# Moving GpSimd's long steps to VectorE and ScalarE, layer-2 SiLU as ScalarE's function, new costs in the order generator, and two table loads

## The chip, the core and the metric

The kernel runs on one core of one Trainium2 chip. A core has five engines that run side by side and wait for each other by semaphores: TensorE (PE, matmuls), VectorE (DVE), ScalarE (ACT), GpSimd (POOL) and SyncE (SP, which issues the transfers). The metric is the device time of one launch in microseconds; lower is better.

## What is computed

A sequence of 2048 frames of width 1024 (float32) passes through two layers and a final RMSNorm. Each layer scales and shifts the normalised frames by a condition vector `c`, mixes them along the sequence, gates them and adds them to the residual stream.

```python
def reference(x, c, ada_w, ada_b, norm_g, final_g, ...):
    c_act = jax.nn.silu(c)
    for i in range(2):
        cond = c_act @ ada_w[i] + ada_b[i]                 # shift, scale, gate: 3 x 1024
        h = rmsnorm(x, norm_g[i]) * (1.0 + scale) + shift
        if i == 0:
            out = rglru_block(h, ...)                      # layer 1
        else:
            out = gated_deltanet_block(h, ...)             # layer 2
        x = x + gate * out
    return rmsnorm(x, final_g)

def rglru_block(h, ...):
    xb, zg = split(h @ in_w)                               # 1024 -> 2 x 1024
    xb = causal_dwconv(xb, conv_w) + conv_b                # 4 taps along the sequence
    r_t, i_t = sigmoid(blockwise(xb) @ gate_w + gate_b)    # 8 blocks of 128
    log_a = -8.0 * r_t * softplus(-lam)
    a_t, b_t = exp(log_a), sqrt(-expm1(2.0 * log_a)) * (i_t * xb)
    hseq = scan(h_t = a_t * h_(t-1) + b_t)
    return (hseq * silu(zg)) @ out_w

def gated_deltanet_block(h, ...):
    q, k, v, z, a_in, b_in = split(h @ in_w)               # 8 heads of 128; z: gate
    q, k, v = silu(causal_dwconv((q, k, v), conv_w))
    q, k = l2norm(q) * 128 ** -0.5, l2norm(k)
    beta, g = sigmoid(b_in), -exp(a_log) * softplus(a_in + dt_bias)
    o = chunk_gated_delta_rule(q, k, v, g, beta)           # state 128 x 128 per head
    return (rmsnorm(o) * onorm_g * silu(z)) @ out_w
```

## The kernel before

**Matmuls in three products.** Each float32 operand of a large matmul is split in an upper half, rounded by a cast to the matmul's reduced type, and a lower half, the operand minus the upper half. PE makes three products of the halves (`products`, L668): upper by upper, upper by lower, lower by upper.

**Tiles and stages.** The sequence is cut in two units (u = 0, 1) of 1024 frames, each unit in two tiles (i = 0, 1) of 512. Layer 1 projects each tile with 16 weight panels of 1024 x 128 (kinds x and z, 8 each), layer 2 with 32 (k, v, q, z). A panel is loaded once per unit (L606), its upper half is cast on ACT (`whi`, L644). In the first unit the lower half is made on POOL (`wlo`, L650) and also stored; in the second unit it is loaded back. A projected tile of 128 x 512 is then worked on by ACT, DVE and POOL while PE goes on:

- layer 1, x: convolution (`convolve`, L746 on ACT, L756 on DVE), halves of the result (`xh` L798 on ACT, `xl` L801 on DVE), gate matmuls (`pg`, L807), sigmoids as tanh on ACT (L857), then `gates_thread`: tanh and exp on ACT (L817, L819), two DVE steps (L821, L823), one POOL step (`th`, L825), DVE (L827), square root on ACT (L830), DVE product (L834), scan on DVE (L838), and the product with the gate `tz` on POOL (L845), then the store to `y_d`.
- layer 1, z: tanh on ACT (L783) and (tanh + 1) times the input on DVE (L785): SiLU, up to a factor of two that the output weights take up.
- layer 2, k, v, q (`conv2_thread`): a copy out of PSUM on ACT (`xe`, L730), the first tap on POOL (`xf`, L997), three taps on DVE (L718), tanh on ACT (L1009) and (tanh + 1) times the input on DVE (L1014). The convolution's weights are halved beforehand (L379), so this is SiLU.
- layer 2, z (`zgate_thread`): tanh (L1023) and a DVE step (L1025), then a store.
- layer 2, keys (`key_thread`): four exponentials of the decays on ACT per tile and head (L1128), transposed keys (`pk`, L1135), their norms with a power on POOL (`rsqrt`, L242 and L243), products of keys (`pkk`).
- layer 2, inverses: a 32 x 32 triangular inverse in 31 pairs of small DVE steps (L1292, L1295), and four rounds of small matmuls.
- layer 2, recurrence: per 128 frames `pp` on PE (L1412, L1413), `zt` on DVE (L1421), `py` on PE (L1429), `yt` on ACT (L1435), `pS` on PE (L1441, L1442), `state` on DVE (L1454).

Where a tile of activations is made for a projection (`split_thread`), ACT scales and shifts it (L561), the upper half is cast on DVE (L569; for the first four on ACT, L566), and the lower half is made on DVE (L575) or, for the first four and for every odd one of the later tiles, on POOL (L572).

At the start, `first_loads_thread` loads the condition's weights (L292) for layer 1 in four pieces, one after the other; two of them go through PE (L328), two through DVE (L353, L355), and PE sums the latter over the partitions (L277). `columns_thread` loads eight small tables (L374) after the second piece and prepares them on DVE (L379 to L389, softplus in L248 to L260); three more small tables come earlier (L303). The later condition rows are summed on DVE (L410).

**What sets the order.** Engines execute their instructions in the order in which the program writes them. That order comes from a generator in the kernel's source (`Weave`): each step of the work is a small thread that asks for an engine with a duration (`yield "dve", 0.33`), for a buffer, or for an event. The generator keeps a time for each engine, always takes the step that can start earliest (by priority where equal), and writes its instruction. After a step, the thread goes on at the step's end plus a lag per engine, or plus a lag given at that place. These durations only set the order; they change nothing in the instructions themselves.

## Time and profile before

| | us |
|---|---|
| runs, lowest, median, highest | 1934.42, 1935.67, 1940.69 |
| span of the profiled execution | 1937.1 |
| busy: PE, DVE, ACT, POOL | 1844.0, 1471.2, 1048.2, 654.8 |

The profile is one execution. "Busy" is the time in which an engine had an instruction in work; matmuls overlap each other, so a busy PE is not a PE at its peak. A line of a group gives the kernel's line, engine, operation, the tile written and the tiles read, the count, busy time, mean duration in nanoseconds, and the idle time of the engine just before with what ended it. A line of the timeline gives the start, the duration, and the same names. Stages by the trace: the start up to 50 us, layer 1 up to 500, its output projection up to 668, layer 2's first unit up to 1240, its second up to 1745, the last projection to the end.

### The profile page before, as it was taken

The numbers are of one execution on the slowest core, as the hardware profiler recorded it, in microseconds if no ns is written. First come the engines' busy times: TensorE is split into PE (matmuls) and PEld (weight loads), VectorE is DVE, ScalarE is ACT, GpSimd is POOL, SyncE is SP. The second block draws the span as 40 slices with busy tenths as digits, with TensorE's granted clock in tenths as the row PEclk, the third lists the DMA queues.
The fourth block names the chain that finished last, engine by engine and source line by source line (L and its number), as shares of the span: only waits on it lengthen the run. The fifth ranks groups of instructions, "written<-read, shape, count | busy, mean of one in ns | idle before, by whom it ended". The sixth has DMA issues, their size and how long they took to land.

```text
span 1937.1 us, 31289 instructions
## 1 busy us (share of the span) xinstructions
PE 1844.0 (95%) x10286; PEld 1503.9 (78%) x10286; DVE 1471.2 (76%) x3175; ACT 1048.2 (54%) x2587; POOL 654.8 (34%) x1116
## 2 busy tenths in 40 slices
PE   6999999999899999898999999999999999999998
PEld 3787778878688877677787877788888888888887
DVE  6898998887544668869888896769777878886653
ACT  3666677667212345375565663565666656654321
POOL 3344542223100235345445543333332334411110
PEclk9999999999899999999999998999999999999999
DMA  8476746554578735446676565555365555687751
GB/s 320 116 219 189 223 138 220 175 167 138 169 204 236 208 106 145 128 111 160 166 186 141 138 158 150 149 156 158 102 163 143 140 140 139 155 246 207 230 161 66
DMA packets 511723, 322.77 MB, mean 167 GB/s; under 512 B 371268, under 2 KB 439236, under 8 KB 511560
## 3 DMA queue, kind: packets, MB, share of 16 engines
q1 hardware_dynamic: 511560, 320.77, 59.1%
q8 instruction: 81, 1.33, 0.3%
q14 instruction: 82, 0.67, 0.1%
HBM read 219.93 MB, written 100.73 MB: 166 GB/s over the span
## 4 chain that ended last, share of the span: by engine, by line
PE 61%; DVE 20%; DMA 6%; issue 4%; ACT 4%; SPq 3%; POOL 2%; DVEq 0%; POOLq 0%; ACTq 0%
PE mm L668 31%; PE mmo L668 16%; DVE xf L718 2%; DVE ttmp L1292 2%; DVE tblk L1295 2%; PE pg L807 1%; PE py L1429 1%; PE pp L1412 1%; PE pS L1442 1%; PE pqk L1257 1%; PE pS L1441 1%; PE pp L1413 1%; PE pkk L1169 1%; DVE xf L756 1%; DMA raw<-in_w 1%
## 5 line engine op out<-in xcount | busy, mean ns | idle before, releaser
L718 DVE SCALAR_TENSOR_TENSOR xf<-xe,cw_s,xf 128x512 f32<-128x512 f32 x288 | 224.9, 784 | 20.6 <-POOL xf L997 18.1
L650 POOL TENSOR_TENSOR wlo<-raw,whi 128x1024 fp32r<-128x1024 f32 x48 | 120.9, 2519 | 143.6 <-ACT whi L644 115.4
L1292 DVE TENSOR_TENSOR ttmp<-blk,tblk 128x60 f32<-128x60 f32 (+24 forms) x496 | 125.4, 253 | 16.6 <-DMA blk<-blk_d 5.4
L1295 DVE TENSOR_TENSOR tblk<-tblk,ttmp 128x60 f32<-128x60 f32 (+24 forms) x496 | 124.8, 252 | 10.7
L644 ACT CAST whi<-raw 128x1024 fp32r<-128x1024 f32 x96 | 100.2, 1044 | 50.3 <-DMA raw<-in_w 44.5
L668 PE MATMUL mmo<-oh,yh 128*128 128x512 f32 x256 | 102.1, 399 | 4.8 <-ACT oh L907 4.8
L668 PE MATMUL mm<-hh_('in2', 0)_5342,whi 128*128 128x512 f32 x256 | 105.3, 411 | 0.0
L668 PE MATMUL mm<-hh_('in2', 0)_5437,whi 128*128 128x512 f32 x256 | 105.3, 411 | 0.0
L668 PE MATMUL mmo<-ol,yh 128*128 128x512 f32 x256 | 102.2, 399 | 3.0 <-DVE ol L909 3.0
L668 PE MATMUL mm<-hh_('in2', 0)_5342,wlo 128*128 128x512 f32 x256 | 104.7, 409 | 0.0
L668 PE MATMUL mm<-hl_('in2', 0)_5343,whi 128*128 128x512 f32 x256 | 104.7, 409 | 0.0
L668 PE MATMUL mm<-hl_('in2', 0)_5438,whi 128*128 128x512 f32 x256 | 104.1, 407 | 0.0
L668 PE MATMUL mm<-hh_('in2', 1)_12030,wlo 128*128 128x512 f32 x256 | 104.1, 407 | 0.0
L668 PE MATMUL mm<-hl_('in2', 1)_12219,whi 128*128 128x512 f32 x256 | 104.0, 406 | 0.0
L668 PE MATMUL mm<-hh_('in2', 0)_5437,wlo 128*128 128x512 f32 x256 | 103.9, 406 | 0.0
L668 PE MATMUL mm<-hh_('in2', 1)_12218,whi 128*128 128x512 f32 x256 | 103.6, 405 | 0.0
L668 PE MATMUL mm<-hh_('in2', 1)_12030,whi 128*128 128x512 f32 x256 | 103.5, 404 | 0.0
L668 PE MATMUL mm<-hl_('in2', 1)_12031,whi 128*128 128x512 f32 x256 | 103.3, 403 | 0.0
L668 PE MATMUL mm<-hh_('in2', 1)_12218,wlo 128*128 128x512 f32 x256 | 103.2, 403 | 0.0
L668 PE MATMUL mmo<-ol,oh 128*128 128x512 f32 (+1 forms) x264 | 103.1, 391 | 0.0
L668 PE MATMUL mmo<-oh,ol 128*128 128x512 f32 (+1 forms) x264 | 103.1, 391 | 0.0
L668 PE MATMUL mmo<-oh,oh 128*128 128x512 f32 (+1 forms) x264 | 103.0, 390 | 0.0
(331 smaller groups left out, 5649.8 us busy)
## 6 DMA issues: line engine op xcount, KB each, us to landing
raw<-in_w SPq DMA_DIRECT2D x96, 512.0 KB, 4.2
araw<-in_ada_w SPq DMA_DIRECT2D x32, 512.0 KB, 4.3
xt<-x_d SPq DMA_DIRECT2D x32, 512.0 KB, 4.9
xt_d<-xb SPq DMA_DIRECT2D x192, 64.0 KB, 2.4
xk<-xt_d SPq DMA_DIRECT2D x24, 512.0 KB, 6.1
xt<-in_x SPq DMA_DIRECT2D x16, 512.0 KB, 4.4
ada<-in_ada_w SPq DMA_DIRECT2D x16, 512.0 KB, 8.5
y_d<-tz SPq DMA_DIRECT2D x32, 256.0 KB, 3.2
```

The source lines that it names most:

```text
L644: act.copy(hi, raw)
L650: pool.tensor_tensor(lo, raw, f(hi), ALU.subtract)
L668: pe.matmul(pt, lhsT=lhs[a][:, k, :], rhs=rhs[b][:, k, :], start=(k == 0 and n == 0), stop=(k == KT - 1 and n == 2))
L718: dve.scalar_tensor_tensor(xf, xe[:, 1 + j:1 + j + TC], wc[:, j:j + 1], xf, ALU.mult, ALU.add)
L756: dve.scalar_tensor_tensor(xf[:, 3:TC], pt[:, j:j + TC - 3], wc[:, j:j + 1], xf[:, 3:TC], ALU.mult, ALU.add)
L807: pe.matmul(pg, lhsT=a[:, g, :], rhs=b, start=(q == 0), stop=(q == 2))
L1169: pe.matmul(pkk[:, b, :], lhsT=kc, rhs=kc, start=True, stop=True)
L1257: pe.matmul(pqk[:, b, :], lhsT=kt[:, b * P:(b + 1) * P], rhs=qt[:, b * P:(b + 1) * P], start=True, stop=True)
L1292: dve.tensor_tensor(tmp, blk[:, j, j + 1:32].unsqueeze(2).to_broadcast([P, r, c_]), t[:, j, 0:c_].unsqueeze(1).to_broadcast([P, r, c_]), A ...
L1295: dve.tensor_tensor(t[:, j + 1:32, 0:c_], t[:, j + 1:32, 0:c_], tmp, ALU.subtract)
L1412: pe.matmul(pp[:, 0, :], lhsT=kc, rhs=S_, start=True, stop=True)
L1413: pe.matmul(pp[:, 1, :], lhsT=qc, rhs=S_, start=True, stop=True)
```

## The change

1. **Work moves.** The lower half of a weight panel, the lower halves of the activations and layer 1's product with the gate go from POOL to DVE. The first tap of layer 2's convolution goes from POOL to ACT. Layer 2's SiLU becomes one ACT instruction with the function Silu, in place of tanh on ACT and a DVE step; the halving of the convolution's weights and of the output norm's factor goes with it. POOL keeps the powers, the carries of the convolution, the masks, one step of layer 1's decay (L825) and the lower half of the gate weights (L875).
2. **Loads at the start.** Eleven small tables become two (`head`, `small`), packed on the host. The first weight panel is loaded before the condition's weights, and these come in alternating pieces for PE and DVE. The tables are prepared on DVE as soon as `c` is spread out.
3. **The generator.** Durations and lags are new numbers throughout. A step named `dve2` or `pool2` is not placed inside a step of the other kind. A step of ACT can name its table ("exp", "silu", "sqrt"); a change of table costs 1.28. PE pays 0.12 where a thread comes to it from a wait. The durations of large matmuls go from 0.2163 (layer 2) and 0.2275 (layer 1) to 0.228.
4. **Small ones.** The first four projections use other PSUM banks, transposes for one slot only alternate banks, and the first panel of layer 2 waits until the output weights of layer 1 have been issued.

```diff
+LAG = {"pe": 0.2, "act": 0.128, "dve": 0.113, "pool": 0.034}
+WEIGHTS = 0.12
+TABLE = 1.28
+SHARED = {"dve2": "pool2", "pool2": "dve2"}
...
-    LAG = {"pe": 0.2, "act": 0.3, "dve": 0.3, "pool": 0.2}
...
+    def engine(self, th, t, kind, dur, lag=None, table=None):
+        e = th.last = kind.rstrip("2")
+        if table is not None and table != self.table:
+            t, self.table = t + TABLE, table
+        if kind in SHARED:
+            for a, b in self.held[SHARED[kind]][-6:]:
+                if a <= t < b:
+                    t = b
+            self.held[kind].append((t, t + dur + (0.08 if e == "dve" else 0.0)))
+        self.free[e] = t + dur
+        th.t = t + dur + (LAG[e] if lag is None else lag)
```

The loads at the start:

```diff
     def first_loads_thread():
-        yield ev("loaded", (("in1", 0), 0))
+        yield ev("firstpanel")
+        for half in range(2):
...
+            for q in range(4):
+                for n in (2 * half, 2 * half + 1):
...
+                    sp.dma_start(out=raws[n % 2][:, 2 * q:2 * q + 2, :], in_=ada_w[0, 2 * part + d, :, 2 * q:2 * q + 2, :])
...
     def first_small_thread():
-        for dst, src in ((c_col, c), (ada_s, ada_c), (norm_s, norm_c)):
-            yield "sp", 8 * KB, dst is c_col
-            sp.dma_start(out=dst, in_=src)
+        yield "sp", 32 * KB, False
+        sp.dma_start(out=head_s, in_=head)
+        w.spawn(arrive_thread(ev("head")), 0)
+        yield "sp", 80 * KB, False
+        sp.dma_start(out=small_s, in_=small)
...
     def columns_thread():
-        yield ev("adaissue", 1)
-        for dst, src in ((cw1_s, cw1), (cb1_s, cb1), (gb_s, gate_b), (lam_s, lam), (cw2_s, cw2), (onorm_s, onorm),
-                         (alog_s, a_log.to_broadcast([P, NH])), (dtb_s, dt_bias.to_broadcast([P, NH]))):
-            yield "sp", 8 * KB, False
-            sp.dma_start(out=dst, in_=src)
...
-        yield ev("cond", 0, 0, 0)
-        yield "dve", 5.75
-        dve.tensor_scalar(cw2_s, cw2_s, 0.5, None, ALU.mult)
+        yield ev("tables")
+        yield ev("cbc")
+        yield "dve2", 3.42
         dve.tensor_scalar(gb_s, gb_s, 0.5, None, ALU.mult)
-        dve.tensor_scalar(onorm_s, onorm_s, 0.5, None, ALU.mult)
```

Activations, weight panels, layer 1's product:

```diff
-        if early or k % 2 and tag == "hf":
-            yield "pool", 1.2
-            pool.tensor_tensor(hl[:, k, :], h, f(hh[:, k, :]), ALU.subtract)
-        else:
-            yield "dve", EV
-            dve.tensor_tensor(hl[:, k, :], h, f(hh[:, k, :]), ALU.subtract)
+        yield "dve2", 0.599
+        dve.tensor_tensor(hl[:, k, :], h, f(hh[:, k, :]), ALU.subtract)
...
-                    yield "pool", 2.3
-                    pool.tensor_tensor(lo, raw, f(hi), ALU.subtract)
+                    yield "dve2", 1.14
+                    dve.tensor_tensor(lo, raw, f(hi), ALU.subtract)
...
-        yield "act", 3.1
+        yield "act", 0.54, LAG["act"], "sqrt"
         act.activation(tr, tr, AF.Sqrt, scale=-0.25)
...
-        yield "pool", 1.4
-        pool.tensor_tensor(tz, tz, ti, ALU.mult)
+        yield "dve2", 0.6
+        dve.tensor_tensor(tz, tz, ti, ALU.mult)
```

Layer 2's convolution, SiLU, gate and exponentials:

```diff
-        yield "pool", 0.68
+        yield "act", 0.535
         xf = tile_([P, TC], "xf", "xf")
-        pool.tensor_scalar(xf, xe[:, 1:1 + TC], cw2_s[:, idx, 0:1], 0.0, ALU.mult, ALU.add)
+        act.activation(xf, xe[:, 1:1 + TC], AF.Copy, scale=cw2_s[:, idx, 0:1])
...
-        yield "act", 0.53
-        tt = tile_([P, TC], "tt", "tt")
-        act.activation(tt, xf, AF.Tanh)
...
-        yield "dve", EV
+        yield "act", 0.533, LAG["act"], "silu"
         r = tile_([P, TC], kind + "t", kind + "t")
-        dve.scalar_tensor_tensor(r, tt, 1.0, xf, ALU.add, ALU.mult)
+        act.activation(r, xf, AF.Silu)
...
-        yield "act", CP
+        yield "act", 0.497, LAG["act"], "silu"
         tz = tile_([P, TC], "tt", "tz")
-        act.activation(tz, pt, AF.Tanh, scale=0.5)
-        yield "dve", EV
-        dve.scalar_tensor_tensor(tz, tz, 1.0, pt, ALU.add, ALU.mult)
+        act.activation(tz, pt, AF.Silu)
...
         for b in range(TB):
-            yield "act", 0.295, 0.0 if b < TB - 1 else 0.3
+            yield "act", 0.299, LAG["act"], "exp"
             act.activation(ec[:, b, :], ec[:, b, :], AF.Exp, bias=gc[:, h, i * TB + b:i * TB + b + 1])
```

More of the change, by code (lines that the diff above doesn't have):

```diff
@@ L121, in run @@
             w, value = th.want, None
+            if t > th.t and not isinstance(w, tuple):
+                th.last = None
             th.t = t
@@ L133, in run, with trunk_kernel @@
             else:
[L134 to L135 removed]
+                self.engine(th, t, *w)
             self.advance(th, value)
 @with_exitstack
[L140 to L141 removed]
+def trunk_kernel(ctx, tc, x, head, small, ada_w, ada_b, final_g, w1, gate_w, ow1, w2, wab, ow2, out):
     nc = tc.nc
@@ L178, in trunk_kernel, with part_of @@
     pool.tensor_tensor(fold[:, 0:16], ident[0:32, 0:16], ident[0:32, 16:32], ALU.add)
+    small_s = cp.tile([P, SMALL], F32, name="small_s")
+    def part_of(tile_in, at, *shape):
+        n = 1
+        for s in shape:
+            n *= s
+        ap = tile_in[:, at:at + n]
+        return ap.rearrange("p (a b) -> p a b", b=shape[1]) if len(shape) == 2 else ap
+    cw1_s, cw2_s = part_of(small_s, 0, KT, 4), part_of(small_s, 32, 24, 4)
+    gb_s, cb1_s = part_of(small_s, 128, 2, KT), part_of(small_s, 144, KT)
+    dtb_s, onorm_s = part_of(small_s, 152, NH), part_of(small_s, 160, 1)
     c_col = cp.tile([P, KT], F32, name="c_col")
@@ L485, in norm_thread @@
         for k in range(KT):
-            bank = "d" if layer == 0 and k % 2 else "tp"
+            bank = "d" if slot == "A" and k % 2 else "tp"
             ptok = yield slots[bank]
-            yield "pe", 4 * TR
+            yield "pe", 0.436
             pt = ps.tile([P, TC], F32, tag=bank, name="tph")
@@ L619, in panels_thread @@
                 if m == 0 and name == ("in1", 0):
-                    for q in panels[0:2]:
-                        ahead.append((yield from panel_load(name, q)))
+                    yield ev("loaded", (("in1", 0), 0))
+                    ahead.append((yield from panel_load(name, panels[0])))
+                    w.set(ev("firstpanel"))
+                    yield ev("adaissue", 1)
+                    ahead.append((yield from panel_load(name, panels[1])))
                     w.set(ev("firstpanels"))
@@ L681, in job @@
         bank = ("d" if layer == 1 else "c") if kind in "vz" else "mm"
+        if name == ("in1", 0) and n < 4:
+            bank = "mm" if n < 2 else "d"
         mtok = yield slots[bank]
         pt = ps.tile([P, TC], F32, tag=bank, name="mm")
-        yield from products(pt, (hi, lo), h, (lambda k: ev("split", (name, i), k)), 0.2275 if layer == 1 else MM)
+        yield from products(pt, (hi, lo), h, (lambda k: ev("split", (name, i), k)))
         if all(q != p for q, _ in jobs[n + 1:]):
@@ L1743, in cols, with table @@
         return a.reshape(a.shape[:-1] + (-1, P)).transpose((a.ndim,) + tuple(range(a.ndim)))
+    def table(*parts):
+        return np.concatenate([np.broadcast_to(p, (P,) + p.shape[1:]).reshape(P, -1) for p in parts], axis=1)
     g = v["gdn_in_w"][0]
```

344 lines of the change are left out of this document (163 added, 181 removed).

## Prediction

> **What bounds the kernel now.** I read the span first, then the busy time by stage, then what TensorE (PE) waited for in each stage, then the groups of VectorE (DVE), ScalarE (ACT) and GpSimd (POOL).
>
> ```profile
> span 1937.1 us, 31289 instructions
> ```
>
> The profiled execution spans 1937.1 us and the median of the runs is 1935.67, so sums are made against 1937.1 and 1.4 us is taken off at the end. Next, the stages: start, layer 1, its output projection, layer 2 first half, second half, last projection. Columns: width, then busy time (instructions) of PE, PE's weight loads, DVE, ACT, POOL, then the granted clock and DMA.
>
> ```profile
> 0.00:50.00 50.00, 30.41 (x105) 17.83 (x105) 34.13 (x75) 19.16 (x32) 18.48 (x33) 0.94 0.81 310
> 50.00:500.00 450.00, 429.72 (x1841) 344.29 (x1840) 389.05 (x575) 306.85 (x439) 173.11 (x152) 0.98 0.59 179
> 500.00:668.00 168.00, 165.38 (x706) 133.42 (x705) 83.49 (x114) 33.85 (x42) 14.01 (x23) 0.99 0.73 209
> 668.00:1240.00 572.00, 531.33 (x3330) 435.19 (x3329) 459.66 (x1149) 320.93 (x964) 263.07 (x456) 0.98 0.57 146
> 1240.00:1745.00 505.00, 501.96 (x3348) 419.78 (x3348) 395.04 (x1113) 311.77 (x972) 165.78 (x395) 1.00 0.58 152
> 1745.00:1937.00 192.00, 185.18 (x965) 153.41 (x963) 109.80 (x154) 55.67 (x139) 20.37 (x59) 0.99 0.54 164
> ```
>
> PE bounds the kernel, and its matmuls are not changed. So a gain can come only from PE's idle time and from the clock that it loses beside it. Idle is width minus PE busy: 19.6, 20.3, 2.6, 40.7, 3.0 and 6.8 us, 93.0 in all. The missing clock times the busy time gives 1.8, 8.6, 1.7, 10.6, 0 and 1.9 us, 24.6 more. Some 118 us is therefore the most that any reordering can win. The two halves of layer 2 do almost the same work (3330 and 3348 matmuls). One loses 40.7 + 10.6 = 51 us, the other 3. What differs: POOL is busy 263 us against 166, and a DVE instruction takes 459.66/1149 = 0.40 us against 0.355.
>
> PE's waits in the first half of layer 2 (us, times, longest), and then those in layer 1:
>
> ```profile
> PE pk L1135 <- DVE kt L1014: 7.6, 4, 3.9
> PE pp L1412 <- DVE state L1454: 6.4, 7, 1.8
> PE py L1429 <- DVE zt L1421: 5.3, 4, 1.9
> ```
>
> ```profile
> PE pg L807 <- DVE xl L801: 6.8, 7, 1.9
> PE mmo L668 <- ACT oh L907: 3.6, 1, 3.6
> ```
>
> PE waits for a late DVE. Why DVE is late shows where both engines' operations stand next to each other:
>
> ```profile
> 29.25 2.36 POOL L650 TENSOR_TENSOR wlo<-raw,whi 128x1024 fp32r<-128x1024 f32 x1 [1.95 <-ACT whi L644]
> 29.32 2.31 DVE L257 TENSOR_TENSOR sp<-sp,sp_d 128x8 f32<-128x8 f32 x1
> 31.57 4.97 POOL L572 TENSOR_TENSOR hl_('in1', 0)_210<-h,hh_('in1', 0)_209 128x512 fp32r<-128x512 f32 x4
> 36.80 0.17 DVE L257 TENSOR_TENSOR sp<-sp,sp_d 128x8 f32<-128x8 f32 x1
> ```
>
> An operation of 8 columns, 0.17 us by itself, ends with POOL's long weight split, after 2.31 us. The POOL groups that the change moves, and how much of the first one falls in the first half of layer 2:
>
> ```profile
> L650 POOL TENSOR_TENSOR wlo<-raw,whi 128x1024 fp32r<-128x1024 f32 x48 | 120.9, 2519 | 143.6 <-ACT whi L644 115.4 <-DMA wlo_d2z<-wlo 8.5 <-DMA xt<-in_x 6.6
> L997 POOL TENSOR_SCALAR xf<-xe,cw_s 128x512 f32<-128x512 f32 x96 | 75.1, 782 | 1.7 <-DMA raw<-in_w 1.5
> L845 POOL TENSOR_TENSOR tz<-tz,tg 128x512 f32<-128x512 f32 x32 | 50.3, 1571 | 0.0
> ```
>
> ```profile
> 668.00:1240.00 572.00, 74.87 (x30) 0.98 0.57 146
> ```
>
> **The change, part by part.** The prices come from these groups:
>
> ```profile
> L1009 ACT ACTIVATE tt<-xf 128x512 f32<-128x512 f32 x96 | 60.5, 631 | 77.7 <-DVE xf L718 75.7 <-DVE tblk L1295 1.3
> L1128 ACT ACTIVATE ec<-ec,gc 128x128 f32<-128x128 f32 x128 | 42.1, 394 | 8.6 <-POOL ec L1124 8.5
> L410 DVE SCALAR_TENSOR_TENSOR acc<-araw,c_col,acc 128x512 f32<-128x512 f32 x56 | 53.6, 958 | 2.8 <-DMA araw<-in_ada_w 2.6
> L821 DVE SCALAR_TENSOR_TENSOR th<-tg,th 128x512 f32<-128x512 f32 x32 | 33.2, 1039 | 15.6 <-ACT tg L819 15.6
> L834 DVE TENSOR_TENSOR tg<-tg 128x512 f32<-128x512 f32 x32 | 26.6, 830 | 0.4 <-ACT tg L830 0.4
> L785 DVE SCALAR_TENSOR_TENSOR tz<-tz,mm 128x512 f32<-128x512 f32 x32 | 21.8, 682 | 8.6 <-ACT tz L783 5.2 <-issue 3.5
> L929 DVE TENSOR_TENSOR yl<-yf,yh 128x1024 fp32r<-128x1024 f32 x16 | 20.5, 1281 | 10.8 <-ACT yh L925 10.7 <-DMA xt_d<-xb 0.2
> ```
>
> *Layer 2, first half.* DVE takes over the weight splits: 30 by 1.28 us (L929, same shape) is +38 us, and some ten odd lower halves of the activations by 0.68 (L785) +7. SiLU leaves DVE: 48 convolutions and 16 gates by 0.68 is -44 us. So the listed work stays level. What goes is the collisions. Each of the 30 splits can hold DVE for up to its 2.5 us, so the bound is 75 us; from below, nothing. The DVE time per instruction says 0.045 x 1149 = 52 us for all collisions together, but this half also holds more long transposes and splits than the other, so I take 40. DVE falls from 460 to about 420 of 572 us. PE's 51 us of idle and slow clock should fall toward the 3 us of the half that has no weight splits on POOL. The same splits still pass ACT, DVE and two weight DMAs each, so I leave 15 us: **-36 us**.
>
> *ACT in both halves.* The first tap adds 48 operations per half by 0.63 (L1009, a ScalarE step over the same tile): +30 us. SiLU takes the place of tanh, at the same 0.63. What the trace of before doesn't show is SiLU's table set: layer 2 ran on one set. In layer 1, ACT changes sets as follows:
>
> ```profile
> 221.48 0.17 ACT L750 COPY edge<-mm 128x6 f32<-128x6 f32 x1
> 221.67 1.28 ACT L830 ACT_TABLE_LOAD   x1
> 222.96 0.63 ACT L830 ACTIVATE tg<-tg 128x512 f32<-128x512 f32 x1
> ```
>
> From the copy's end at 221.65 to the square root's start at 222.96 are 1.31 us. A half holds 64 exponentials (L1128) in 16 groups of four, and 64 SiLUs. If SiLU shared the set with exponential there would be no load; with each group in one piece there are 32; with strict alternation 128. I take 50 per half, nearer to whole groups since each group stands together in the code: 50 x 1.31 = 66 us. ACT's second half becomes 312 + 30 + 66 = 408 of 505 us, 81%; DVE at 78% left PE 3 us idle there. Behind each load wait on ACT's queue the copy that empties a projection's PSUM bank and the copy of py that the state update on PE needs; both have a filling of projection matmuls. I take **+4 us** in the second half, bounds -3 and +30.
>
> The Trainium skill prices this higher: ScalarE: Activation LUTs, section What ACT_TABLE_LOAD costs, gives 1283 ns plus a drain of about 1380 ns, 2.66 us for every switch. The 1283 agrees with the trace; the drain does not show in the rows above. By the page 50 loads would be an estimated 133 us per half and ACT 94% full.
>
> *Layer 1.* DVE gets 16 weight splits by 1.28 (+20), 32 products with the gate by 0.68 (+22) and eight lower halves (+5): +47 us on 389 of 450. It loses collisions: L821 at 1.039 and L834 at 0.830 stand against 0.682 for L785, which reads PSUM. Four such two-input operations per tile, at 0.15 to 0.36 us too much, 32 tiles: 19 to 46 us, of which I take 32; the 56 steps of the condition (L410) at 0.958 give up to 56 x 0.28 = 15 more. So DVE stays level. The gain is in latency: a weight split is ready 1.2 us after its cast in place of 2.5, and the product 0.7 after the scan in place of 1.6. Some POOL work that collides is left (the tensor_scalar of the decay, the gate weights). Of 20.3 + 8.6 us I take off less than half: **-12 us**, bounds +10 (DVE at 97%) and -24.
>
> *Start.* The small tables hold the queue of SP and then DVE:
>
> ```profile
> 19.36 0.33 SPq L374 DMA_DIRECT2D dtb_s<-in_dt_bias  x1
> 19.73 0.91 SPq L606 DMA_DIRECT2D raw<-in_w  x2
> ```
>
> ```profile
> 35.95 0.79 PE L668 MATMUL mm<-hh_('in1', 0)_209,whi 128*128 128x512 f32 x1
> 39.12 0.48 DVE L353 TENSOR_SCALAR acc<-ada,c_col 128x512 f32<-128x512 f32 x1
> 46.20 1.18 PE L277 MATMUL adac<-ones,acc 128*128 128x1 f32 x8 [4.22 <-DVE acc L355]
> ```
>
> The first projection matmul runs at 35.95. The accumulation for the second half of the condition begins on DVE at 39.12, after the preparation of the tables, and PE waits for it until 46.20. Two table loads instead of eleven let SP issue the first panel before the condition's weights instead of at 19.73, and DVE prepares the tables while those weights are on their way. The lower halves that PE needs first leave POOL (four, the 4.97 us that follow the split at 29.25) for DVE at 0.68. I expect the first projection matmul near 28 and the second half's at 38 in place of 50: **-12 us**. If the transfers bound it, which bring the same condition weights and rows of x as before, half of it is left; -17 if all of the 19.6 and 1.8 goes but what the first loads take.
>
> *The rest.* Output projection and last projection: no POOL work of weight is taken out, their waits are 2.6 and 6.8 us, the latter mostly the end after the last matmul: 0. The order is written anew with other costs. By itself it moves no work, and I give it no term: it is what turns a freed DVE into a PE that does not wait, and it can also turn against it (rivals). Of the moves, each store follows its producer: the kept weights wait on SP for DVE instead of POOL, about 1.2 us earlier, and the product's store 0.9 us earlier.
>
> POOL keeps its powers, and these also run beside DVE:
>
> ```profile
> 882.55 1.01 POOL L243 TENSOR_TENSOR ro<-so,mhalf 128x4 f32<-128x4 f32 x1
> 882.59 0.25 DVE L1292 TENSOR_TENSOR ttmp<-blk,tblk 128x66 f32<-128x66 f32 x1
> 882.87 0.23 DVE L1295 TENSOR_TENSOR tblk<-tblk,ttmp 128x66 f32<-128x66 f32 x1
> ```
>
> Two DVE operations with two inputs pass at 0.25 and 0.23 us while the power runs for 1.01, so what stays on POOL costs DVE little. The Trainium skill, SBUF — State Buffer, section Who interferes with whom, has the shared port held for the whole instruction by whichever engine started first; the trace disagrees for this short operation. By the page each power would still hold DVE for up to its 1 us.
>
> **Sum.** -36 + 4 - 12 - 12 = -56; 1937.1 - 56 = 1881, less 1.4: **1880 us**.
>
> **Rivals.**
> *A. Nearly all the waits go.* If both halves of layer 2 run like the second (-48), the start gives -17 and layer 1 -24, it is -89: 1847 us. For it: the second half at 3 us of idle with DVE at 78%. Against it: layer 1 keeps DVE at 86%, in series with ACT and the scan.
>
> *B. The collisions were not what PE waited for.* The 40.7 us could come from the chain key, inverse, recurrence, which has to fill when layer 2 begins, and the matmuls would have to wait for it anyway. Then a third of -36 is left, and start and layer 1 give half: -12 - 6 - 6 = -24, 1912 us. For it: the longest single waits are for `kt` and `state`, both links of that chain. Against it: they end at DVE.
>
> *C. ACT becomes the bound of layer 2, slower than before.* The new order puts SiLUs between the exponentials of a group; every such place costs two loads. At 128 loads per half, 168 us, ACT has 321 + 30 + 168 = 519 and 312 + 30 + 168 = 510 us to do. Kept 90% busy, the halves last 577 and 567 us: +5 and +62, with -24 from the rest +43: 1978 us. It decides from about 100 loads per half on, where ACT passes 93% of the second half. By the page's price for a switch that point would lie near 50 loads. For it: layer 1 mixes square roots so; L783, L817 and L830 there carry loads of their own. Against it: the generator charges for a load, and the four exponentials stand together.
>
> *D. Nothing measurable.* The new order loses in the second half, where before hardly anything was lost, what the first wins; 1936 us. For it: 505 us with 3.0 idle can hardly be met twice. Against it: a loss of over 40 us there needs a bound engine, which is C.
>
> **How the numbers follow.** What a measurement of this kernel can tell from no change is 0.3%, 5.8 us. My forecast, taken as 1862 to 1900, has 0.48; A, under 1862, 0.20; B, 1900 to 1930, 0.16; D 0.05; C 0.11. Faster: 0.48 + 0.20 + 0.16 = 0.84. The range goes from 1838, a little under A's sum, to 1930, the upper end of B. It leaves out C, D and the tail of A.
>
> **What would show it.** Right: the rows of L718 and of the inverse's steps in the first half at the times that they have in the second; PE idle there under 20 us at a clock of 0.99 or more; no POOL operation over 1.3 us; the first projection matmul before 30 us; 30 to 70 table loads in each half of layer 2. Wrong: over 100 loads per half with PE waiting for ACT's copies of py or of the projections (C); the collisions gone but PE idle over 25 us in the first half, still behind `kt` and `state` (B); the second half of layer 2 more than 15 us longer (C or D); layer 1 not shorter, with DVE over 95% busy there.

## The result, and the profile after

| | before | after |
|---|---|---|
| median of 4 runs | 1935.36 us (1934.42 to 1940.69) | 1915.61 us (1908.93 to 1920.17) |
| after over before | | 0.9886, 95% interval 0.9858 to 0.9914 |
| profiled run, its span | 1937.1 us | 1911.45 us, 1909.7 us |

The change is faster, as forecast, but by 20 us (1.1%, with the interval below 1) and not by 55. By the profiled executions the span lost 27.4 us of the 56 in the sum. These are the stages of the changed kernel, cut at the first projection matmul of each (columns as in the table of stages above: width, busy time of PE, its weight loads, DVE, ACT and POOL, then clock and DMA):

```profile
0.00:50.00 50.00, 35.59 (x131) 22.61 (x131) 35.17 (x86) 21.72 (x38) 11.28 (x30) 0.93 0.83 331
50.00:258.00 208.00, 194.06 (x838) 155.71 (x837) 179.90 (x302) 130.86 (x201) 34.77 (x50) 0.98 0.61 183
258.00:473.00 215.00, 207.32 (x899) 167.72 (x898) 173.15 (x291) 150.80 (x209) 31.39 (x41) 0.98 0.52 167
473.00:668.00 195.00, 185.49 (x787) 147.84 (x786) 110.69 (x162) 49.03 (x63) 12.52 (x23) 0.99 0.73 210
668.00:1184.00 516.00, 503.57 (x3260) 413.81 (x3260) 387.31 (x1086) 374.11 (x1026) 137.49 (x362) 1.00 0.61 155
1184.00:1708.00 524.00, 516.34 (x3428) 423.81 (x3427) 367.09 (x1084) 392.31 (x1077) 125.88 (x351) 1.00 0.56 147
1708.00:1909.70 201.70, 191.27 (x954) 156.77 (x952) 112.69 (x148) 57.90 (x132) 19.63 (x55) 0.99 0.54 170
```

And the same cuts for the kernel before; its first row is the one quoted in the prediction:

```profile
50.00:265.00 215.00, 203.71 (x872) 163.03 (x871) 193.07 (x283) 139.54 (x213) 101.79 (x88) 0.98 0.63 186
265.00:476.00 211.00, 207.82 (x902) 167.17 (x901) 176.06 (x269) 150.24 (x207) 62.24 (x57) 0.99 0.54 168
476.00:668.00 192.00, 183.57 (x775) 147.51 (x774) 103.41 (x139) 50.92 (x63) 23.09 (x30) 0.97 0.73 209
668.00:1217.00 549.00, 510.24 (x3192) 418.56 (x3191) 441.87 (x1111) 304.22 (x920) 250.88 (x440) 0.98 0.57 144
1217.00:1734.00 517.00, 512.19 (x3428) 427.37 (x3427) 402.67 (x1126) 320.29 (x997) 174.68 (x407) 1.00 0.58 150
```

Layer 1 ends at 473 in place of 476: start and layer 1 together won 3 us. Its output projection lost 3. The first half of layer 2 won 33, the second lost 7, the last projection won 1.

Where the 33 us came from stands in the groups of DVE in the first half of layer 2, before and then after (last columns: busy time, mean ns of one, idle time ahead):

```profile
L718 DVE SCALAR_TENSOR_TENSOR xf<-xe,cw_s,xf 128x512 f32<-128x512 f32 x144 | 116.3, 811 | 13.5 <-POOL xf L997 12.1
L1295 DVE TENSOR_TENSOR tblk<-tblk,ttmp 128x54 f32<-128x54 f32 x16 | 6.9, 432 | 0.3
```

```profile
L742 DVE SCALAR_TENSOR_TENSOR xf<-xe,small_s,xf 128x512 f32<-128x512 f32 x144 | 106.6, 747 | 22.1 <-ACT xf L1021 20.5
L672 DVE TENSOR_TENSOR wlo<-raw,whi 128x1024 fp32r<-128x1024 f32 x30 | 36.6, 1219 | 8.6 <-ACT whi L666 8.5
L1306 DVE TENSOR_TENSOR tblk<-tblk,ttmp 128x54 f32<-128x54 f32 x16 | 3.4, 214 | 0.4
```

Unchanged operations got shorter: a tap 811 to 747 ns, an inverse step of 54 columns 432 to 214. The 30 weight splits came to DVE at 1.22 us, where 1.28 were taken. DVE's work in this half fell by 55 us, and PE's idle time (width minus PE busy) from 38.8 to 12.4. What PE still waits for longest there (us, times, longest) is small:

```profile
PE py L1440 <- DVE zt L1432: 2.1, 2, 1.7
```

ACT's table loads in layer 2 are 69, which these groups show nearly whole:

```profile
L1139 ACT ACT_TABLE_LOAD x32 | 41.1, 1283 | 0.6
L1028 ACT ACT_TABLE_LOAD x28 | 35.9, 1283 | 0.4
L1036 ACT ACT_TABLE_LOAD x7 | 9.0, 1283 | 0.1
```

About 35 per half: on the mean one load for each of the 32 groups of four exponentials, and about as many for SiLU. Some groups stand together, some are broken by a SiLU. Over the whole execution, what PE waits for most is now in layer 1 and at the start:

```profile
PE mm L690 <- DVE xf L780: 14.1, 3, 7.8
PE adaps L359 <- DMA ada<-in_ada_w: 12.1, 1, 12.1
```

### The profile page after: what moved, and what is told of

The parts are those of the page before. It is cut to its first block, busy times and chain, and to the rows that moved or that the text cites. A ratio compares the mean times of both kernels' runs of the same rounds, so it can differ in the third digit from the quotient of the medians.

```text
span 1909.7 us, 31149 instructions
## 1 busy us (share of the span) xinstructions
PE 1833.6 (96%) x10286; PEld 1488.3 (78%) x10286; DVE 1366.0 (72%) x3153; ACT 1176.7 (62%) x2743; POOL 373.0 (20%) x912
## 5 line engine op out<-in xcount | busy, mean ns | idle before, releaser
L742 DVE SCALAR_TENSOR_TENSOR xf<-xe,small_s,xf 128x512 f32<-128x512 f32 x288 | 213.4, 748 | 40.4 <-ACT xf L1021 37.2
L690 PE MATMUL mm<-hh_('in2', 0)_5265,whi 128*128 128x512 f32 x256 | 104.5, 408 | 0.0
L690 PE MATMUL mm<-hh_('in2', 1)_12035,whi 128*128 128x512 f32 x256 | 104.4, 408 | 0.0
L690 PE MATMUL mm<-hl_('in2', 1)_12036,whi 128*128 128x512 f32 x256 | 104.0, 406 | 0.2 <-DVE hl_('in2', 1)_12036 L592 0.2
L690 PE MATMUL mm<-hl_('in2', 1)_12218,whi 128*128 128x512 f32 x256 | 103.9, 406 | 0.0
L690 PE MATMUL mm<-hh_('in2', 1)_12217,wlo 128*128 128x512 f32 x256 | 103.9, 406 | 0.0
L690 PE MATMUL mm<-hh_('in2', 1)_12035,wlo 128*128 128x512 f32 x256 | 103.8, 405 | 0.0
L690 PE MATMUL mm<-hh_('in2', 1)_12217,whi 128*128 128x512 f32 x256 | 103.7, 405 | 0.0
L690 PE MATMUL mm<-hh_('in2', 0)_5436,wlo 128*128 128x512 f32 x256 | 103.6, 405 | 0.0
L690 PE MATMUL mm<-hh_('in2', 0)_5265,wlo 128*128 128x512 f32 x256 | 103.5, 404 | 0.0
```

Source lines behind the costliest of these rows:

```text
L690: pe.matmul(pt, lhsT=lhs[a][:, k, :], rhs=rhs[b][:, k, :], start=(k == 0 and n == 0), stop=(k == KT - 1 and n == 2))
L742: dve.scalar_tensor_tensor(xf, xe[:, 1 + j:1 + j + TC], wc[:, j:j + 1], xf, ALU.mult, ALU.add)
```

## The experiments

All medians stand beside runs of the kernel before on the same chip, so each comes with its ratio to that. "Order kept" means that only the engine of one step is changed and all else stands where it stands in the changed kernel; where the order is written anew, the generator was run again. Of a profiled execution, "PE idle" is width minus busy.

**Parts taken back, order kept.** First the lower halves of the weights on GpSimd again:

```diff
-                    dve.tensor_tensor(lo, raw, f(hi), ALU.subtract)
+                    pool.tensor_tensor(lo, raw, f(hi), ALU.subtract)
```

> The order of the changed kernel is kept instruction for instruction; only the 48 lower halves of the weight panels are made on GpSimd again. Theory 1 (the collisions of this split with VectorE were the loss of layer 2's first half, and moving it off GpSimd is nearly the whole gain): that half gets 20 to 35 us longer, layer 1's first unit 3 to 8, the run 1938 to 1958 us. Theory 2 (the new order made the gain, the place of the split matters little): 1912 to 1925 us.

1938.84 us, ratio 1.002 (0.9996 to 1.0044): 23 us more than after, so these 48 steps alone undo the gain, in an order that was written for them on VectorE. The split takes 2.495 us again, and the first half of layer 2 is 535 us, 19 more than in after and just short of the 20 to 35 expected. The taps of this half get longer again, beyond what they took in before (last line):

```profile
L672 POOL TENSOR_TENSOR wlo<-raw,whi 128x1024 fp32r<-128x1024 f32 x48 | 119.8, 2495 | 185.4 <-ACT whi L666 153.7 <-DMA pq<-q_d 12.1 <-ACT edge L774 7.7
```

```profile
678.00:1213.00 535.00, 510.54 (x3257) 417.90 (x3256) 391.08 (x1054) 373.60 (x1023) 204.94 (x392) 0.98 0.58 149
```

```profile
L742 DVE SCALAR_TENSOR_TENSOR xf<-xe,small_s,xf 128x512 f32<-128x512 f32 x144 | 121.5, 852 | 33.4 <-ACT xf L1021 32.0
```

DVE is busy 391 us here without the 30 splits. In after it is busy 387 us with them, 350.7 without: the same other steps take 40 us longer while the splits run on GpSimd. That is the collisions' price, apart from the split's own longer time. Against after's row PE is idle 12 us longer, and busy 7 us longer at a clock of 0.98 for 1.00: here idle time and a lower clock come together.

Second, SiLU as tanh and a VectorE step, which takes the 69 table loads away:

```diff
-        act.activation(r, xf, AF.Silu)
+        act.activation(r, xf, AF.Tanh)
+        dve.scalar_tensor_tensor(r, r, 1.0, xf, ALU.add, ALU.mult)
```

(and likewise for the gate, with the convolution's and the norm's factors halved).

> The order is kept; layer 2's SiLU is again tanh on ScalarE and a step on VectorE, written in the place of the Silu instruction (and the two halvings of tables at the start). Table loads in layer 2 go from 69 to 1 or 2, VectorE gets 128 steps of 0.68 us, 87 us. Theory A (the table loads cost the second half the 7 us that it lost): that half shortens by 4 to 10 us and the run to 1905 to 1912. Theory B (VectorE's time is worth more than ScalarE's, the loads are hidden): layer 2 gets longer by 5 to 25 us, 1920 to 1940.

1953.43 us, ratio 1.0101 (1.0082 to 1.0119), 38 us more than after and beyond the 1920 to 1940 of Theory B, with one load left in layer 2. The halves take 543 and 542 us, 27 and 18 more than in after; ACT has 40 us less to do and DVE 38 more in each:

```profile
666.00:1209.00 543.00, 512.95 (x3261) 413.49 (x3260) 426.12 (x1151) 333.54 (x994) 135.84 (x362) 0.99 0.57 147
```

```profile
PE pp L1427 <- DVE state L1469: 10.3, 19, 1.1
```

PE waits for DVE's links of the chain many times for half a microsecond. In this order the 69 loads, 88 us of ACT, are worth it: PE hardly waits behind them (1.0 us at most for a SiLU in after's layer 2), and it does behind DVE's steps. An order written for tanh with the rest of the work as in after was not run.

Third, the first tap on GpSimd again:

```diff
-        act.activation(xf, xe[:, 1:1 + TC], AF.Copy, scale=cw2_s[:, idx, 0:1])
+        pool.tensor_scalar(xf, xe[:, 1:1 + TC], cw2_s[:, idx, 0:1], 0.0, ALU.mult, ALU.add)
```

> The whole computation; the order is that of after, instruction for instruction, only the first tap of each of layer 2's 96 convolutions is again GpSimd's (0.78 us each) instead of ACT's (0.72). Theory 1 (what matters of GpSimd's work is the two-input steps, which hold VectorE's two-input steps; a one-input step of GpSimd does not): VectorE's taps stay within 3% of after's 748 ns, and the two halves of layer 2 move by less than 8 us in either direction: 1908 to 1924 us. Theory 2 (any long step of GpSimd beside VectorE costs): VectorE's taps take 780 ns or more as in before, and the run is over 1928 us. A third outcome, a gain of more than 8 us, would say that ACT, 75% busy in the second half, was what it is short of.

1929.9 us, ratio 0.9953 (0.993 to 0.9975), 14 us more than after. DVE's taps take 760 ns on the mean, within 3% as by the first theory; the run is over 1928 us, as by the second. So this one decides nothing between them. On the collisions the kernel before has more to say: in its second half of layer 2 the first taps run on GpSimd too, but no weight splits, and the taps take 757 ns (750 in after's second half). So the one-input step hardly held VectorE there; where the 14 us come from stays open. The third outcome is out: the second half of layer 2, in which ACT has 29 us less to do, takes 531.8 us, 7 to 8 more than in after, so in this order it was not short of ACT.

**The start.** Half of the first condition's weights is not loaded, the first two tiles are used again:

```diff
             for q in range(4):
                 for n in (2 * half, 2 * half + 1):
+                    if half:
+                        w.set(ev("adaload", n, q))
+                        continue
```

> Leaves out part of the computation: the second half of the first layer's first condition weights (two tiles of 2.1 MB) is not loaded, and the first half's two tiles stand in for it, so half of layer 1's condition has other values; every matmul and every VectorE step of the start is still there. Theory 1 (the start is bound by transfers, 15.2 MB in 40 us without a pause, and therefore did not get 6 us shorter): 4.2 MB less at about 414 GB/s is 10 us; the first projection matmul goes from 35.7 to 26 to 30 us, the wait of TensorE for the condition weights (12.1 us) falls below 6, and the run is 5 to 10 us shorter than after, 1901 to 1909 us by its median of 1915.6 us. Theory 2 (TensorE's and VectorE's chain from the sums of the condition to the first scaled panel binds, and the weights would have been in time): the first projection matmul stays within 2 us of 35.7 and the run within 3 us of after.

1903.9 us, ratio 0.9847 (0.9825 to 0.9869): 12 us less than after by the medians, 6 by the profiled spans. The median lies in the first theory's range, but not by its mechanism: the first projection matmul, its main number, did not move forward (37.24 us), and PE is idle 14.8 us of the first 50 as against 14.4 in after. Layer 1 ends 4 us earlier, at 469; where the rest of the gain came from isn't shown. The order at the start is another one here (the second half's sum stands ahead of the projection). The transfers now pause at 31 us, and PE's rows show why that helps nothing, first in the changed kernel and then in this one:

```profile
12.12 2.05 PE L359 MATMUL adaps<-ada,c_bc 128*128 128x512 f32 x2 [12.12 <-DMA ada<-in_ada_w]
...
24.25 1.05 PE L299 MATMUL adac<-ones,acc 128*128 128x1 f32 x8 [1.45 <-DVE acc L386]
...
27.19 1.12 PE L512 MATMUL tph<-ident,xt 128*128 128x128 f32 x4 [0.85 <-ACT h L582]
...
35.69 0.79 PE L690 MATMUL mm<-hh_('in1', 0)_246,whi 128*128 128x512 f32 x1
...
40.31 0.95 PE L299 MATMUL adac<-ones,acc 128*128 128x1 f32 x8
```

```profile
12.08 2.04 PE L362 MATMUL adaps<-ada,c_bc 128*128 128x512 f32 x2 [12.08 <-DMA ada<-in_ada_w]
...
25.44 1.05 PE L299 MATMUL adac<-ones,acc 128*128 128x1 f32 x8 [1.44 <-DVE acc L389]
...
37.24 0.79 PE L693 MATMUL mm<-hh_('in1', 0)_239,whi 128*128 128x512 f32 x1
```

Between the first weights at 12.12 and 35.69 PE is idle for 1.45 + 0.85 us; the other 21.3 are the condition's sums and the transposes that stand ahead of the projection in its order. In after the start is bound by the arrival of the first weights and then by PE's own queue.

**Layer 1.** Up to 231 us PE stands 7.8 us for a PSUM bank that the convolution (L780) frees. DVE's rows ahead of that, in order:

```profile
218.42 1.28 DVE L845 SCALAR_TENSOR_TENSOR th<-tg,th 128x512 f32<-128x512 f32 x2
219.62 1.83 DVE L847 SCALAR_TENSOR_TENSOR tg<-th 128x512 f32<-128x512 f32 x2
221.37 2.11 DVE L851 SCALAR_TENSOR_TENSOR tg<-tg,xf 128x512 f32<-128x512 f32 x2
225.78 1.54 DVE L431 SCALAR_TENSOR_TENSOR acc<-araw,c_col,acc 128x512 f32<-128x512 f32 x2 [2.29 <-DMA araw<-in_ada_w]
227.23 1.22 DVE L672 TENSOR_TENSOR wlo<-raw,whi 128x1024 fp32r<-128x1024 f32 x1
228.36 3.49 DVE L780 SCALAR_TENSOR_TENSOR xf<-mm,small_s,xf 128x509 f32<-128x509 f32 x5
```

DVE waits 2.29 us for a condition row (`araw`) that nobody needs yet, and the split and the convolution stand behind it. I tried two ways to give that row time, both with the order written anew. In the first, every row's load gets a margin of 4.8 us:

```diff
                 sp.dma_start(out=raw, in_=ada_w[layer, 2 * part + d, :, 2 * q:2 * q + 2, :])
+                yield "none", 2 * MARGIN
```

> The generator counts 4.8 us more for the landing of each piece of the condition rows in layer 1 before it places VectorE's steps on it; all work is that of the changed kernel, the order is written anew. Theory 1 (VectorE waits in order for these pieces, the convolution behind them holds a PSUM bank, and TensorE's three waits of 14 us in layer 1 follow from that): those waits fall under 5 us and layer 1 gets 6 to 14 us shorter, 1901 to 1910 us. Rival (the waits come from VectorE's load or from the PSUM banks, wherever the rows stand): layer 1 within 4 us, 1911 to 1922.

1931.34 us, ratio 0.9986 (0.9974 to 0.9999). The first half of layer 1 came down as expected, but the run missed its 1901 to 1910. The last steps of the rows came later (623 us in place of 505), and PE stands 16.3 us between layer 1's output projection and layer 2; the second half of layer 2, newly written, takes 551 us:

```profile
50.00:242.00 192.00, 189.29 (x833) 152.89 (x832) 169.75 (x287) 129.95 (x197) 34.34 (x50) 1.00 0.62 183
460.00:664.50 204.50, 185.32 (x796) 149.38 (x795) 108.90 (x158) 36.20 (x45) 10.94 (x23) 0.95 0.73 213
```

```profile
PE mm L691 <- DVE hh_('in2', 0)_5458 L591: 16.3, 1, 16.3
```

That wait is not for layer 2's condition, whose last shift and scale are ready at 523 us. PE stops at 648, and the tile `hh` that it waits for comes from rows of x that land from their transfer at 663. What put this transfer so late in the new order isn't shown.

In the second the margin is only for layer 1's own two rows (`if layer == 0:` ahead of it):

> The whole computation. The margin of 4.8 us between a condition row's load and the steps that use it is given only to the two rows of layer 1's own gate, that is the 8 loads in the first half of layer 1's projections; the order from there on is written anew. Theory 1: the first half goes from 222.7 to 207 to 213 us, the last row of layer 2's condition starts within 20 us of where it does in after (449 us), so the output of layer 1 keeps its 194 us instead of 204; 8 to 15 us are won if the newly written order of layer 2 is as good as after's, 1900 to 1908 us. Theory 2 (each newly written order draws its own waits, and those of layer 2 are larger than what is won here): layer 1 gains as above, but the two halves of layer 2 add more than 10 us, and the run is at 1915 to 1935 us.

**1899.91 us, ratio 0.9827 (0.9804 to 0.985)**: better than both kernels. From 50 us the first half of layer 1 takes 192.6 us in place of 208, with 2.6 us idle, and layer 2 keeps its times:

```profile
50.00:242.60 192.60, 189.99 (x836) 153.40 (x836) 171.35 (x289) 130.43 (x198) 34.23 (x50) 1.00 0.62 183
653.60:1168.50 514.90, 504.03 (x3260) 414.87 (x3259) 388.87 (x1089) 375.26 (x1027) 137.59 (x362) 0.99 0.60 156
```

Was it the row's transfer, or the place of the convolution? With the order kept, the rows' loads left out, and their steps reading the identity tile in place of the row:

```diff
-                sp.dma_start(out=raw, in_=ada_w[layer, 2 * part + d, :, 2 * q:2 * q + 2, :])
...
-                        dve.scalar_tensor_tensor(acc, raw[:, k, :], ck, acc, ALU.mult, ALU.add)
+                        dve.scalar_tensor_tensor(a4, i4, ck, a4, ALU.mult, ALU.add)
```

> Leaves out part of the computation: the 30 loads of condition rows (512 KB each, read while layer 1 runs) are not made, and the 64 row steps of VectorE read a tile that is always there, so the gates of layer 1 and layer 2's condition have other values; the order of everything else is that of after, and the weight tiles no longer share their buffers with the rows. Theory 1 (VectorE stands in order behind a row's transfer, and TensorE then waits for the convolution that stands behind it): the waits of TensorE for the convolution (14.1 us in after) fall below 3 us, the first half of layer 1's projections goes from 222.7 to 208 to 213 us and the second from 215.2 to 209 to 213, and the run is 10 to 20 us shorter than after: 1896 to 1906 us. Theory 2 (the convolution is late because VectorE, at 86% busy there, has too much to do): the two stages stay within 4 us of after, and so does the run. Layer 2 should stay where it is by both, 516 and 525 us, within 5.

1909.13 us, ratio 0.9877 (0.9848 to 0.9906); the first half from 50 us takes 202.8 us. The transfer's wait on DVE is gone, and PE still waits:

```profile
225.14 0.77 PE L689 MATMUL mm<-hh_('in1', 0)_246,whi 128*128 128x512 f32 x1 [5.31 <-DVE xf L779]
```

So 5 of the 15 us belong to the transfer. The other 10 came only with the newly written order: in after the convolution is written behind the gate's steps (L845 to L851) and the row's. My first theory of this wait was right in a third.

**The generator's constants.** The prediction gave the newly written order no term. Two runs split work from order. The first has the new order generator, loads and banks, with before's work on before's engines (the splits, lower halves, products and first taps on GpSimd, SiLU as tanh and a VectorE step):

```diff
-                    yield "dve2", 1.14
-                    dve.tensor_tensor(lo, raw, f(hi), ALU.subtract)
+                    yield "pool2", 2.34
+                    pool.tensor_tensor(lo, raw, f(hi), ALU.subtract)
...
-        yield "act", 0.535
+        yield "pool2", 0.69
```

> The generator, the loads and the banks of the changed kernel with the work of the kernel before: weight splits, odd lower halves, product with the gate and first tap on GpSimd, SiLU by tanh and VectorE; the generator knows their traced times and the shared port. Theory 1 (the place of the work makes the gain): 1925 to 1945 us, the first half of layer 2 at 540 us or more. Theory 2 (the order makes it): 1900 to 1920 us, that half at 525 or less.

The second has after's work with the four constants of before:

> The whole computation with the work where after has it; only the four constants of the order generator are those of before (results are seen 0.3, 0.3 and 0.2 us behind ACT, VectorE and GpSimd, no time for TensorE's weight load, none for the table load, no shared port). Theory 1 (the gain comes from where the work is done, and the generator's latencies are worth little by themselves): the first half of layer 2 stays below 535 us (516 in after, 549 in before), GpSimd's busy time is that of after, and the run lies between 1905 and 1930 us. Theory 2 (the latencies and the table time carry the gain; without them the 69 table loads become some 150 and ACT becomes the bound): table loads above 120, ACT above 430 us in one half of layer 2, and the run at 1945 us or more.

```diff
-LAG = {"pe": 0.2, "act": 0.128, "dve": 0.113, "pool": 0.034}
-WEIGHTS = 0.12
-TABLE = 1.28
-SHARED = {"dve2": "pool2", "pool2": "dve2"}
+LAG = {"pe": 0.2, "act": 0.3, "dve": 0.3, "pool": 0.2}
+WEIGHTS = 0.0
+TABLE = 0.0
+SHARED = {}
```

1970.5 us (ratio 1.0186, 1.017 to 1.0203) and 2020.16 us (1.0449, 1.043 to 1.0468). Each half of the change alone is slower than before; both together are faster. Of the first run's theories the first had the half of layer 2 right (553 us) and the time wrong; the second run came as its Theory 2 said by the time, but with 71 table loads and not 120. The place of the work alone does not make the gain. Then one constant at a time, the line `TABLE` alone and the line `LAG` alone:

> The whole computation with the work where after has it; of the generator's constants only the 1.28 us of a table load are set to nothing, so it plans a SiLU or an exponential as if no load stood before it. With all four constants old the run was at 2020.2 us, with 71 loads, TensorE idle 78 us in the halves of layer 2 (20 in after) in many short waits, 16 of them behind the SiLU of the keys. Theory 1 (the waits come from results that arrive a table load later than planned): the waits behind the SiLU of the keys come back, both halves of layer 2 get 10 to 40 us longer, the run is at 1940 to 1985 us. Theory 2 (the latencies behind each engine carry it, set too long before): the run stays within 10 us of after (1915.6), the SiLU waits stay under 5 us.

> The whole computation with the work where after has it; of the generator's constants only the three latencies are those of before (0.3, 0.3 and 0.2 us behind ACT, VectorE and GpSimd in place of 0.128, 0.113 and 0.034), so it plans each step of a chain 0.17 to 0.19 us later than it can start. Theory 1 (table load): the run stays within 15 us of after, 1900 to 1930. Theory 2 (latencies): the chains of the recurrence are planned late and shifted against each other, the halves of layer 2 add 20 us or more each, the run is at 1955 us or more.

2002.46 us (ratio 1.0336, 1.0312 to 1.0361) and 2014.96 us (1.04, 1.0372 to 1.0427). Either alone costs 87 to 99 us, the first more than its Theory 1 had. The loads stay near 70, so it isn't their number. Without the table load's time PE waits where SiLU comes later than planned, and in the recurrence behind ACT too:

```profile
PE pk L1146 <- ACT kt L1028: 17.4, 11, 4.2
PE pS L1452 <- ACT yt L1446: 13.3, 17, 1.8
```

With the old latencies it waits in the recurrence, some 20 times a link, and the clock falls to 0.93:

```profile
646.60:1210.50 563.90, 517.61 (x3121) 428.14 (x3120) 367.05 (x1015) 373.56 (x991) 127.09 (x354) 0.93 0.55 140
```

```profile
PE py L1440 <- DVE zt L1432: 10.9, 18, 2.2
PE pS L1452 <- ACT yt L1446: 10.8, 23, 1.3
```

**Is an order a draw?** Each newly written order might land anywhere. So six more, each by a small change of a constant that should hardly matter: three orders of the changed kernel, two of the kernel before, and one of the old work under the new generator. The edits are these, one for each run (the margin's serves three runs, `SEEN`'s two):

```diff
-MARGIN = 2.4
+MARGIN = 2.6
...
-    SEEN = 0.92
+    SEEN = 1.0
...
-LAG = {"pe": 0.2, "act": 0.128, "dve": 0.113, "pool": 0.034}
+LAG = {"pe": 0.2, "act": 0.14, "dve": 0.124, "pool": 0.037}
```

> The whole computation; the changed kernel with the generator's margin at 2.6 us in place of 2.4, which writes a new order. Theory 1 (the constants that were traced make good orders, and a small change of another does little): 1900 to 1935 us, TensorE idle in the halves of layer 2 below 35 us together. Theory 2 (each order is a draw, and the one of after a lucky one): over 1950 us, with waits behind the keys' SiLU or the recurrence as in the run without the table load's time.

> The whole computation; the changed kernel with the generator's time from a transfer's end to its use at 1.0 us in place of 0.92, which writes a new order. Theory 1: 1900 to 1935 us. Theory 2 (a draw): over 1950 us.

> The whole computation; the changed kernel with the three traced latencies a tenth higher (0.14, 0.124 and 0.037 us in place of 0.128, 0.113 and 0.034), which writes a new order. Theory 1 (0.17 to 0.19 us too much cost 99 us, so 0.003 to 0.012 too much cost little): 1900 to 1940 us. Theory 2 (a draw): over 1950 us.

> The whole computation; the kernel before with the generator's margin at 2.6 us in place of 2.4, which writes a new order. Theory 1 (orders by one set of constants lie close together): 1925 to 1960 us. Theory 2 (the order of before is a lucky one among orders that spread widely): over 1970 us, as the old work did under the new generator.

> The whole computation; the kernel before with the generator's time from a transfer's end to its use at 1.0 us in place of 0.92, which writes a new order. Theory 1 (the order of before is a lucky one; its like lie some 35 us higher): 1955 to 1990 us. Theory 2 (the other order, with 1972.6 us, is the outlier): 1925 to 1950 us.

> The whole computation; the old work under the new generator, new loads and new banks, as in the run with 1970.5 us, with the margin at 2.6 us in place of 2.4, which writes a new order. Theory 1 (orders of the old work lie around 1955 to 1985 us by either generator; the work's place, not the generator, separates them from 1900 to 1934): 1950 to 1990 us. Theory 2 (the new generator is good for either work and the 1970.5 us were a bad draw): 1900 to 1940 us.

| work, generator's constants | medians of its orders, us |
|---|---|
| before, before | 1935.4, 1946.68 (ratio 1.0069, 1.0044 to 1.0093), 1972.64 (1.0179, 1.0151 to 1.0207) |
| before, after | 1970.5, 1997.44 (1.0316, 1.028 to 1.0352) |
| after, before (all or one) | 2020.16, 2002.46, 2014.96 |
| after, after | 1915.6, 1917.45 (0.989, 0.9873 to 0.9908), 1923.14 (0.9926, 0.9909 to 0.9943), 1934.12 (0.9989, 0.9974 to 1.0004) |

The three other orders of the changed kernel came as their first theories said. Of the kernel before, one was over 1970 (the second theory there), and the other showed that this one is the outlier; the old work under the new generator came slower than either theory. The orders of one work under one set of constants spread over 18 to 37 us. The 87 to 105 us of the wrong constants are far beyond that, and a difference of 20 us between two orders can be a draw. The changed kernel itself, run once more beside three of these, gave 1915.43 us (0.9896, 0.9875 to 0.9916).

## Why the direction was right and the size twice too large

Two of the four terms failed, the start's and layer 1's, 24 us of the 56. The measured 1915.6 us lie in rival B's band and near its 1912, but that is luck: B keeps most of the waits of layer 2's first half, and these went.

*First half of layer 2, -36: right, -33.* The mechanism is shown by the splits put back, which cost 23 us with the order kept, 19 of them in this half, and by the taps, 747 ns without the splits beside them and 852 with. The other 14 of the 33 us are not split further. DVE fell by 55 us where 40 were taken. Rival B falls with it: PE's idle time is 12.4 us, not over 25, and no link of the chain holds it for more than 1.7 us at a time.

*Second half, +4: +7.* ACT has 392 us to do, by 408 forecast, with 35 loads, not 50. PE's idle time rose by 3 us; the other 4 are busy time on the same 3428 matmuls, which I can't place. Rival C, ACT as the bound, did not come: neither 68 loads fewer nor the first tap off ACT made this half shorter, with the order kept. By the Trainium skill (ScalarE: Activation LUTs, What ACT_TABLE_LOAD costs) a drain of about 1380 ns would go with each load; the rows above have 0.6 us of idle time ahead of all 32 loads of L1139 together, so it doesn't show here either.

*Start, -12: -5.* The step that failed is "I expect the first projection matmul near 28". It came at 35.69, and its time was the wrong measure. In the kernel before, PE stood idle only in these places up to 36 us:

```profile
10.31 3.75 PE L328 MATMUL adaps<-ada,c_bc 128*128 128x512 f32 x4 [10.31 <-DMA ada<-in_ada_w]
24.79 1.05 PE L277 MATMUL adac<-ones,acc 128*128 128x1 f32 x8 [2.70 <-DVE acc L355]
26.40 3.65 PE L328 MATMUL adaps<-ada,c_bc 128*128 128x512 f32 x4 [0.55 <-DMA ada<-in_ada_w]
```

Of the 25.6 us from 10.31 to 35.95, 22.4 are PE's own work, so 28 could not be reached with that work ahead. Of the 19.6 us idle in the first 50, 10.3 were the first weights' arrival: 9.3 were to be had. The 4.2 and 1.8 us around the second half of the condition went (its sum runs at 40.31, not 46.20), and the first weights came 1.8 later, behind the two tables: 19.6 to 14.4.

*Layer 1, -12: about +2.* With the start's 5 us taken off, layer 1 did not get shorter; PE's idle time in it rose from 14.5 to 21.6 us. The step that failed is "DVE stays level. The gain is in latency". The latencies came as priced: in layer 1 the weight split took 1.23 us in place of 2.5, the product 0.71 in place of 1.57. DVE did not stay level but fell, from 369 to 353 us (from 50 us on). Still PE waited, 14.1 us in three places for a convolution, a wait that the kernel before does not have. What decided was neither DVE's load nor the latencies: it was what the written order put ahead of the convolution, as the margin for two rows shows, with 2.6 us idle in that half in place of 13.9. The prediction priced what each step takes and not what stands behind it on an engine that works in order. The other orders say how far that is this one order's affair. Cut at the first projection matmuls of the stages, worked out from each trace, in us:

| order | layer 1 ends | layer 2, first half | second half |
|---|---|---|---|
| before; its two other orders | 476; 480, 475 | 549; 556, 555 | 517; 528, 523 |
| after; its three other orders | 473; 466, 472, 465 | 516; 526, 528, 522 | 524; 532, 541, 538 |
| rows of layer 1 with a margin | 460 | 515 | 526 |

On the means of the three and the four, the first half of layer 2 gains 30 us, the second loses 12, layer 1 ends 8 earlier, and the rest gains 4: 30 us in all, near the 27 of the two profiled runs. So the shortfall is no bad luck of this order: before's was the best of its three, and after's the best of its four. In the order of the last row layer 1 ends 16 us earlier than in before. Five of these are the start's, so layer 1 can give about 11 of the 12 us where the convolution doesn't come late; the forecast of -12 was the price of a possibility.

*No term for the new order: wrong.* With the work where after has it, the constants alone make 87 to 105 us, more than any one step that moved (14 to 38 us, order kept). What stays open is why the new generator, with its loads and banks, suits the new work and costs the old work some 30 us on the mean (1984 of two orders against 1952 of three); the runs show that it does, not why.

## What to carry to other kernels

Bound a gain by the idle time of the engine that sets the time, place by place, before pricing steps: an event that comes earlier gains nothing while that engine is working through its queue. Where a program writes the order, its table of costs is part of the kernel: change it together with the work, and judge a change by several orders, since two orders of the same work lay up to 37 us apart here. In an order that is followed strictly, look at what stands behind a load that nobody needs yet; a margin for two loads was worth 16 us of the median.

## What the runs showed of the hardware

Idle time of PE came with a lower clock, though not in proportion. With the latencies of before alone, the granted clock of layer 2's first half was 0.93 at 46 us idle; it was 0.98 in before at 39, 0.99 with tanh at 30 and 1.00 in after at 12. In the first of these PE was busy 1057 us (517.61 + 539.39) in layer 2's halves, for 1020 in after. With 30 weight splits of 2.4 us on GpSimd in layer 2's first half and the order kept, VectorE's taps there took 852 ns on the mean in place of 747. A table load of ACT took 1.283 us, 69 times in layer 2, and where the plan knew of it PE waited 1.0 us at most behind a SiLU. ACT's copies, scaled copies and squares beside SiLU and exponential took no load of their own: the loads stand only at the exponentials, the SiLUs and, twice, at the softplus.
